# Small constants in one load, hH straight from x, and a front part with three engines' order written by hand

## The chip, the cores and the metric

One core of a Trainium2 chip runs the kernel. The metric is the device time of one execution in microseconds (us); before the change the median of three runs is 948.08 us (947.59 to 949.36).

## The reference

One layer of a hybrid backbone for two groups of tokens with the same weights: 128 prompt tokens and 512 latent tokens, 1024 channels. The part that the change touches is the beginning:

```python
def modulation(cond, w_ada, b_ada):
    mod = jax.nn.silu(cond) @ w_ada + b_ada
    return jnp.split(mod, 3, axis=-1)

def layer_forward(x, cond, ctx_kv, p):
    shift, scale, gate = modulation(cond, p["w_ada"], p["b_ada"])
    h = x * (1 + scale) + shift
    (v_h, x1, x0, g_h), (q, k, v, g_a), m = split_projection(h, p["w_in"], p["conv_w"], p["conv_b"])
    h_fwd, h_bwd = hyena_filters(x.shape[1], ...)
    y_h = hyena_long_conv(v_h, x1, x0, h_fwd, h_bwd, p["hyena_d"])
    ...

def hyena_filters(L, f_w1, f_b1, f_w2, f_b2, f_w3, f_freq):
    ...
    hf = jnp.sin(f_freq[0] * (z @ f_w1 + f_b1))
    hf = jnp.sin(f_freq[1] * (hf @ f_w2 + f_b2))
    hf = (hf @ f_w3).astype(jnp.float32).reshape(L, 2, D_HYENA)
    ...
```

Behind it come a gated long convolution by DFTs, a windowed attention with context keys, the merge of both branches, an output projection and a layer norm. All of it is in 32-bit floating point.

## The kernel before

**Layout.** Channels lie on the 128 partitions, tokens along the free axis: 640 columns, first the 128 of the prompt (PC), then the 512 latent ones (SC). The 1024 input channels are eight k-tiles. A weight tile `i` holds 128 output channels against all eight k-tiles (128 x 1024, 512 KB).

**Precision.** A 32-bit product is built from three matmuls. Each operand is split into a high half H, the value rounded to the matmul's format, and a low half L, the rest: `split` (L90-93) copies on ACT (ScalarE, L92) and subtracts on DVE (VectorE) or POOL (GpSimd) (L93). `accumulate` (L150-157) then runs, for one weight tile and one k-tile, the passes wh·hH, wh·hL, wl·hH, each in two halves of 320 columns: six matmuls at L154. In this text that is a tile-step, written as tile and k-tile (01: tile 0, k-tile 1). A whole tile is eight tile-steps.

**The front part, `prologue` (L240-310).** For each k-tile k it makes the modulation and the modulated input:

- two loads `ada` (512 KB each, one with the shift and one with the scale columns) into one of three buffers X, W, F in turn, so the loads of k+3 wait until the matmuls of k have read theirs; 16 small matmuls each, `adaT` (L235);
- `row` on ACT copies their sums out of PSUM (L267); four matmuls with `sel` turn them to one value per partition, `modT` (L285); DVE adds the bias, `mod` (L289);
- DVE makes `hx = x * scale + shift` from the load `xt` (L295); ACT copies it to `hH[k]` (L92); `hL[k]` is subtracted on POOL for even k and on DVE for odd k (L93).

Between these steps a `script` puts tile-steps of the tiles 0, 8 and 1 on TensorE (PE), as soon as their `hH`, `hL` and weight halves can be there. Tile 9 is loaded and split at the end, together with the first filter weights `w3`, the decays `dec` and the DFT matrices `draw`.

**The filter's two sine layers** (`hidden1`, `hidden2`, `sin_layer`, L195-218) are called whole at k=0 and k=1: two matmuls `ps_f` (L201), nine instructions on DVE (`arg`, `turns`, L202-207), a sine on ACT (L208). `hid` (L217, L218) is what the filters of all quarters are made of.

**What sets the order.** Inside `manual_schedule(engines={PE})` TensorE's instructions of the prologue stand as they are written; a scheduler orders the other engines, and everything behind the prologue, by its own estimate. All loads go through SP's queue in the order written (`keep_in_program_order` in `load_to`, L56-60), but for five small ones on ACT's queue (L184, L187). Landings are counted with eight semaphores used in turn, so a load is issued when the one eight places before it has landed.

**Small constants.** `cc`, `bss`, `sel`, `convw`, `hyd`, `ident` are loads of their own on SP, one put behind each of the first `ada` loads (`smalls`); `zemb`, `fw1`, `fs1`, `fw2`, `fs2` are loads on ACT's queue.

**Behind the prologue.** `quarter_head` runs tile 9, then the tiles 2, 10, 3, 11 and so on. From tile 2 on, `wtile` with `eng="dma"` writes -raw to `wl` on ACT (L132), adds the weights onto the rounded value by an accumulating load from POOL's queue (L133), and makes `wh` on ACT (L134). `dft_consts` splits the DFT matrices into `dftH`, `dftL`; `filter_spectrum(0)` starts with `w3s`, `w3h`, `w3l`, then the matmuls `fz` (L355) and `fl` (L365, L366), which read `hid`. `zs` (L447-451) are ACT's copies of a finished tile out of PSUM, `u` and `x` the short convolution.

Of the kernel before, what the change touches and what calls it, by code (L numbers as in the profile page):

```python
# [9 lines left out]
F32 = mybir.dt.float32  # L10
F32R = mybir.dt.float32r
AF = mybir.ActivationFunctionType
ALU = mybir.AluOpType
# [18 lines left out]
T_Q, T_K, T_V, T_GA, T_MH, T_MA, T_BH, T_BA, T_WO = 32, 40, 48, 56, 64, 72, 80, 88, 96  # L32

# [6 lines left out]
def tile_hyena_natten_step(ctx: ExitStack, tc: tile.TileContext, a, o):  # L40
# [55 lines left out]
    smalls = []  # L96

    def load(name, shape):
        out[name] = const.tile(shape, F32, tag=name, name=name)
        smalls.append((out[name][:], a[name]))  # L100

# [3 lines left out]
    cc = const.tile([P, NK, 2], F32, tag="cc", name="cc")  # L105
    load_to(cc[:], a["cc"])
# [4 lines left out]
    mod = const.tile([P, 2, NK, 2], F32, tag="mod", name="mod")  # L111
# [39 lines left out]
    def accumulate(ps, w, k, xh, xl):  # L151
        for wt, x, first, last in ((w[0], xh, True, False), (w[0], xl, False, False), (w[1], xh, False, True)):
            for hf in range(2):
                nc.tensor.matmul(  # L154
                    ps[hf][:, :HALF], wt[k], x[:, hf * HALF : (hf + 1) * HALF],
                    start=(first and k == 0), stop=(last and k == NK - 1), skip_group_check=True,
                )
# [13 lines left out]
    out = {"yh": {}}  # L171
# [10 lines left out]
    def hidden_loads():  # L182
        out["zemb"] = temp("u", "zemb", 4)[:33]
        nc.scalar.dma_start(out["zemb"], a["zemb"])  # L184
        for name, shape in (("fw1", [33, 64]), ("fs1", [64, 2]), ("fw2", [64, P]), ("fs2", [P, 2])):
            load(name, shape)
            nc.scalar.dma_start(*smalls.pop())  # L187


# [5 lines left out]
    def sin_layer(n, fs, w, src, dst):  # L195
        ar = temp("e", f"arg{n}")[:n]
        kr = temp("plus", f"turns{n}")[:n]
        for hf in range(2):
            hs = slice(hf * 320, hf * 320 + 320)
            ps = aux(f"ps_f{n}{hf}")  # L200
            nc.tensor.matmul(ps[:n, :320], w[:], src[:, hs], start=True, stop=True)  # L201
            nc.vector.tensor_scalar(ar[:, hs], ps[:n, :320], fs[:n, 0:1], fs[:n, 1:2], op0=ALU.add, op1=ALU.mult)  # L202
        nc.vector.tensor_scalar(kr, ar, 1.0 / (2 * math.pi), MAGIC, op0=ALU.mult, op1=ALU.add)
        nc.vector.tensor_scalar_add(kr, kr, -MAGIC)
        for c in (C1, C2, C3):
            nc.vector.scalar_tensor_tensor(ar, kr, -c, ar, op0=ALU.mult, op1=ALU.add)
        nc.vector.tensor_scalar(ar, ar, 3.1415925, -3.1415925, op0=ALU.min, op1=ALU.max)
        nc.scalar.activation(dst, ar, AF.Sin)  # L208

    def hidden1():  # L210
        out["hf1"] = temp("u", "hf1", 4)[:64]
        sin_layer(64, out["fs1"], out["fw1"], out["zemb"], out["hf1"])

    def hidden2():
        hf2 = temp("minus", "hf2")[:]
        sin_layer(P, out["fs2"], out["fw2"], out["hf1"], hf2)
        nc.scalar.activation(hid[:], hf2, AF.Copy)  # L217
        nc.vector.tensor_tensor(hid[64:], hf2[64:], f(hid[64:]), op=ALU.subtract)  # L218
# [3 lines left out]
    ccf = cc[:].rearrange("p k c -> p (k c)")  # L222
    nc.scalar.activation(th0[:], ccf, AF.Tanh, scale=0.5)
    nc.vector.scalar_tensor_tensor(th0[:], th0[:], 1.0, ccf, op0=ALU.add, op1=ALU.mult)
# [3 lines left out]
    def ada(ch, ps, raw):  # L228
        load_to(raw, a["wada"][ch])
        if smalls:  # L230
            load_to(*smalls.pop(0))
# [8 lines left out]
    def prologue():  # L240
        script = (
            ("", "", "", ""), ("00", "", "", ""), ("", "80", "01", "81"), ("", "", "02", "82"),
            ("", "10 11", "03", "83"), ("", "12 13", "04", "84"), ("", "14", "05", "85"), ("", "15", "06", "86 16 07 87 17"),
        )

        def work(k, step):
            for item in script[k][step].split():
                i, j = int(item[0]), int(item[1])
                accumulate(banks[i], early[i], j, hH[:, j], hL[:, j])
# [5 lines left out]
        hidden_loads()  # L255
        for n in ("bss", "sel"):
            load(n, a[n].shape)
        for n in ("convw", "hyd", "ident"):
            load(n, a[n].shape)
        for k in range(NK):  # L260
            psa = aux(f"adaT{k}")
            wt = hw.tile([P, 2048], F32, tag="XWFXWFXW"[k], name=f"ada{k}")
            for part in range(2):
                ada(part * 8 + k, psa[:, part * P : part * P + P], wt[:, 1024 * part : 1024 * part + 1024])
                work(k, part)
            row_ = hwa.tile([P, 2 * P], F32, tag="fb", bufs=2, name=f"row{k}")
            nc.scalar.activation(row_[:], psa[:, : 2 * P], AF.Copy)  # L267
            if k == 0:
                nc.vector.tensor_scalar_add(out["bss"][:, 1], out["bss"][:, 1], 1.0)
            xt = row(yhp, "yh", f"xt{k}")  # L270
            load_to(xt[:], a["xT"][:, k])
            if k == 0:
                begin(0)
            if k == 1:
                begin(8)
            if k == 2:
                w1 = [row(yhp, "yh", f"w1_{i}", F32R)[:, :512] for i in range(4)]
                begin(1, (w1[:2], w1[2:]), (aux("mm1lo"), aux("mm1hi")))
            if k == 7:
                w9 = hw.tile([P, 2, 1024], F32R, tag="X", name="w9")  # L280
                early[9] = wtile(9, dst=([w9[:, 0]], [w9[:, 1]]))
            work(k, 2)
            psm = aux(f"modT{k}")
            for c in range(2):
                nc.tensor.matmul(  # L285
                    psm[:, c * 2 : c * 2 + 2], row_[:, c * P : c * P + P], out["sel"][:, 0:2],
                    start=True, stop=True, skip_group_check=True,
                )
            nc.vector.tensor_tensor(  # L289
                mod[:, :, k, :], psm[:, 0:4].rearrange("p (s c) -> p s c", s=2),  # L290
                out["bss"][:, :, k : k + 1].to_broadcast([P, 2, 2]), op=ALU.add,
            )
            hx = hwa.tile([P, NT], F32, tag="cv", bufs=2, name=f"hx{k}")
            for c, s0, n in ((0, PC, LP), (1, SC, LS)):
                nc.vector.tensor_scalar(  # L295
                    hx[:, s0 : s0 + n], xt[:, s0 : s0 + n], mod[:, 1, k, c : c + 1], mod[:, 0, k, c : c + 1],
                    op0=ALU.mult, op1=ALU.add,
                )
            split(hH[:, k], hL[:, k], hx[:], nc.vector if k % 2 else nc.gpsimd)
            if k < 7:  # L300
                work(k, 3)
            if k == 0:
                hidden1()
            if k == 1:
                hidden2()
        load_filter(0)
        out["dft"] = hw.tile([P, 2560], F32, tag="F", name="draw")
        for i in range(2):
            load_to(out["dft"][:, i * 1280 : i * 1280 + 1280], a["dft"][:, i * 1280 : i * 1280 + 1280])
        work(7, 3)  # L310
# [32 lines left out]
    def filter_spectrum(q):  # L343
# [15 lines left out]
        hyd = out["hyd"][:, 2 * q : 2 * q + 2]  # L359
        nc.vector.scalar_tensor_tensor(hyd, pb0[:, :2], -DECAY0, hyd, op0=ALU.mult, op1=ALU.add)  # L360
# [135 lines left out]
    def long_conv(q):  # L496
        us, F, ident = out[f"u{q}"], out[f"F{q}"], out["ident"]

        def src(cls):
            ps = aux(f"ut{q}_{cls}")  # L500
            for i in range(2):
                s = us[i][:, GAP + cls : NG : 4] if cls < 4 else us[i][:, :LP]
                nc.tensor.transpose(ps[:, i * P : i * P + P], s, ident[:])  # L503
# [47 lines left out]
    def long_conv_back(q):  # L551
        us, ident, hyd, R, W = out[f"u{q}"], out["ident"], out["hyd"], out[f"R{q}"], out[f"W{q}"]
# [34 lines left out]
        for i in range(2):  # L587
            nc.tensor.transpose(outp[:, i * P : i * P + P], yp[:, i * P : i * P + P], ident[:])
        for i in range(2):
            up = us[i][:, :LP]  # L590
            nc.vector.scalar_tensor_tensor(
                up, up, hyd[:, 2 * q + i : 2 * q + i + 1], outp[:, i * P : i * P + P], op0=ALU.mult, op1=ALU.add
# [582 lines left out]
```

## Time and profile before

| what | us |
|---|---|
| median of three runs | 948.08 |
| the profiled execution | 949.61 |
| its span, first to last instruction | 947.7 |
| PE busy | 921.4 |
| DVE, ACT, POOL busy | 469.9, 375.8, 153.8 |
| first matmul starts | 5.75 |
| last tile-steps of the prologue start | 60.24 |
| tile 9 on PE | 63.44 to 70.74 |

The profile is one execution. Each row of a timeline has the start and duration in us, the engine, the line of the code, the operation, what is written from what (names without numbers) and its shape, the number of merged instructions, and in brackets how long the engine had been idle before it and what ended that. SPq, ACTq and POOLq are queues that issue loads; PEld is the load of weights into the array, which overlaps with matmuls. A table of stretches gives the busy time of each engine within it. PEclk is the share of the full TensorE clock that was granted. The loads of the front part, by issue and landing (us):

| load | issued | landed |
|---|---|---|
| first half of `ada` for k=0 | 1.17 | 5.61 |
| `xt` for k=0 | 5.63 | 9.04 |
| first half of `ada` for k=1 | 6.47 | 13.90 |
| second half of `ada` for k=6 | 31.22 | 35.74 |
| second half of `ada` for k=7 | 36.18 | 41.67 |
| `raw` of tile 2 | 39.82 | 47.90 |
| second half of `draw` | 43.31 | 51.85 |

### The profile page before, as it was taken

To read this page: it belongs to the slowest core of one execution; us is meant where nothing else is said; L and a number is where in the kernel's file an instruction comes from. 1 tells how busy PE (TensorE), PEld (TensorE's weight loads), DVE (VectorE), ACT (ScalarE), POOL (GpSimd) and SP (SyncE) were. 2 spreads that over 40 slices of the span, in tenths; PEclk is the share of its full clock that TensorE was granted. 3 is DMA by queue.
4 is the path that set the end of the run, shared out by engine and by line. 5 is a ranking of instruction groups with operands and counts; after the bars stand their busy time and mean duration, and the time that the engine had idled before them with its cause. 6 is when DMAs were issued, how large, how long until landed. Compare 5 with 4: busy or idle time off the path is not lost.

```text
span 947.7 us, 16408 instructions
## 1 busy us (share of the span) xinstructions
PE 921.4 (97%) x6732; PEld 868.3 (92%) x6732; DVE 469.9 (50%) x839; ACT 375.8 (40%) x759; POOL 153.8 (16%) x190
## 2 busy tenths in 40 slices
PE   5989999999999999999999999999999999999996
PEld 3889999999999999988888889989999999999885
DVE  5548685793795775333333332332271223325686
ACT  3266454554554324254444443443361112223300
POOL 1110010110110000464445544213100000000000
PEclk9899999999999999999999999999999999999999
DMA  8865564555565212322222221221212433223631
GB/s 314 315 174 117 125 142 100 134 133 117 119 141 120 71 56 73 113 80 70 68 74 68 63 68 54 76 70 46 68 52 82 135 133 112 72 84 108 204 111 67
DMA packets 38482, 102.57 MB, mean 108 GB/s; under 512 B 5287, under 2 KB 14951, under 8 KB 38408
## 3 DMA queue, kind: packets, MB, share of 16 engines
q1 hardware_dynamic: 33840, 86.69, 28.9%
q0 software_dynamic: 4032, 14.68, 9.5%
q8 instruction: 53, 0.87, 0.4%
q10 hardware_dynamic: 536, 0.16, 0.1%
q14 instruction: 21, 0.17, 0.1%
HBM read 97.85 MB, written 3.67 MB: 107 GB/s over the span
## 4 chain that ended last, share of the span: by engine, by line
PE 89%; DVE 2%; ACT 1%; DMA 1%; issue 0%; POOL 0%; POOLq 0%; DVEq 0%; ACTq 0%
PE mm L154 62%; PE out L1010 6%; PE v L680 5%; PE s L741 3%; PE o L785 3%; PE pt L778 2%; PE ve L689 1%; DMA raw<-wall 1%; DVE wl L93 1%; PE yb L142 1%; PE yb L143 1%; PE yb L141 1%; PE ut L503 0%; PE fl L365 0%; PE fl L366 0%; ACT wh L92 0%
## 5 line engine op out<-in xcount | busy, mean ns | idle before, releaser
L154 PE MATMUL mm<-hH,wh 128*128 128x320 f32 x1120 | 266.1, 317 | 2.2 <-ACT mh L883 1.1
L154 PE MATMUL mm<-hL,wh 128*128 128x320 f32 x1120 | 259.2, 310 | 2.1 <-POOL hL L93 2.1
L154 PE MATMUL mm<-hH,wl 128*128 128x320 f32 x1120 | 260.3, 311 | 0.8 <-DVE wl L93 0.8
L154 PEld LDWEIGHTS mm<-hH,wh 128*128 128x128 f32 x1120 | 185.9, 189 | 10.8 <-issue 6.9
L154 PEld LDWEIGHTS mm<-hL,wh 128*128 128x128 f32 x1120 | 188.7, 189 | 3.1 <-POOL hL L93 2.7
L154 PEld LDWEIGHTS mm<-hH,wl 128*128 128x128 f32 x1120 | 188.8, 189 | 2.2 <-DVE wl L93 1.6
L93 DVE TENSOR_TENSOR wl<-raw,wh 128x1024 fp32r<-128x1024 f32 x66 | 81.3, 1231 | 194.0 <-ACT wh L92 194.0
L92 ACT ACTIVATE wh<-raw 128x1024 fp32r<-128x1024 f32 x66 | 70.0, 1060 | 178.1 <-PE mm L154 99.6
L133 POOL DMA_DIRECT2D wl<-wall x28 | 24.4, 872 | 230.0 <-ACT wl L132 188.1
L762 POOL TENSOR_SCALAR p<-p,sm 128x384 f32<-128x384 f32 x32 | 43.7, 1376 | 46.8 <-DVE sm L761 46.8
L134 ACT ACTIVATE wh<-raw 128x1024 fp32r<-128x1024 f32 x28 | 29.7, 1062 | 46.6 <-PE mm L154 46.6
L780 ACT ACTIVATE pts<-pt 128x384 f32<-128x384 f32 x64 | 28.0, 491 | 35.9 <-PE pt L778 35.9
L1040 POOL TENSOR_TENSOR r<-r,bc 128x64 f32<-128x64 f32 x1 | 0.3, 319 | 249.5 <-ACT r L1039 249.5
L757 DVE CUSTOM_DVE_ANT_0 p<-s,tm 128x384 f32<-128x384 f32 x32 | 16.7, 556 | 44.6 <-PE s L741 44.6
L760 ACT ACTIVATE p<-p,sm 128x384 f32<-128x384 f32 x32 | 19.5, 612 | 47.0 <-DVE sm L757 47.0
L762 POOL TENSOR_SCALAR edge<-edge,sm 128x320 f32<-128x320 f32 x32 | 34.4, 1085 | 16.0 <-PE mm L154 8.8
L455 DVE SCALAR_TENSOR_TENSOR x<-zs,convw,x 128x641 f32<-128x641 f32 x32 | 28.3, 885 | 5.7 <-ACT x L453 5.6
L132 ACT ACTIVATE wl<-raw 128x1024 fp32r<-128x1024 f32 x28 | 30.1, 1076 | 2.0 <-DMA raw<-wall 2.0
L757 DVE CUSTOM_DVE_ANT_0 edge<-s,tm 128x320 f32<-128x320 f32 x32 | 14.6, 489 | 31.3 <-PE s L741 27.1
L154 PE MATMUL mm<-yhH,wh 128*128 128x320 f32 x128 | 29.9, 315 | 0.0
L741 PE MATMUL s<-k,q 64*128 64x320 f32 (+2 forms) x160 | 29.4, 461 | 0.0
L154 PE MATMUL mm<-yhH,wl 128*128 128x320 f32 x128 | 29.2, 310 | 0.1
(312 smaller groups left out, 1662.6 us busy)
## 6 DMA issues: line engine op xcount, KB each, us to landing
raw<-wall SPq DMA_DIRECT2D x96, 512.0 KB, 3.7
wl<-wall POOLq DMA_DIRECT2D x28, 512.0 KB, 5.7
ada<-wada SPq DMA_DIRECT2D x16, 512.0 KB, 6.3
gate<-wada SPq DMA_DIRECT2D x8, 512.0 KB, 3.7
wo<-wall SPq DMA_DIRECT2D x8, 512.0 KB, 3.7
xt<-xT SPq DMA_DIRECT2D x8, 320.0 KB, 6.6
dec<-decay SPq DMA_DIRECT2D x20, 128.0 KB, 3.4
x<-xB SPq DMA_DIRECT2D x5, 512.0 KB, 5.6
```

The lines of the kernel that those rows point to most:

```text
L92: hi = nc.scalar.activation(dst_h, src, AF.Copy)
L93: return hi, (eng or nc.vector).tensor_tensor(dst_l, src, f(dst_h), op=ALU.subtract)
L132: nc.scalar.activation(wl, raw[:], AF.Copy, scale=-1.0)
L134: nc.scalar.activation(wh, raw[:], AF.Copy)
L154: nc.tensor.matmul(ps[hf][:, :HALF], wt[k], x[:, hf * HALF : (hf + 1) * HALF], start=(first and k == 0), stop=(last and k == NK - 1), skip ...
L455: nc.vector.scalar_tensor_tensor(d, zs[:, c : c + NG], convw[:, i, c : c + 1], d, op0=ALU.mult, op1=ALU.add)
L680: nc.tensor.matmul(ps[:, t // 2, t % 2 * 256 : t % 2 * 256 + 256], x[:, k, P * t : P * t + P], wk, start=first and t % 2 == 0, stop=last, ...
L741: nc.tensor.matmul(dst, q[rows(h)], k[rows(h)], start=True, stop=True, skip_group_check=True)
L757: nc.vector.tensor_tensor_reduce(pv, s[h][:, : hi - lo], tm[h][:, lo:hi], 1.0, 3.0e38, ALU.add, ALU.min, accum_out=sm[:, 0:1])
L762: nc.gpsimd.tensor_scalar_mul(pv, pv, sm[:, 2:3])
L785: nc.tensor.matmul(dst, lhs, rhs, start=start, stop=stop, skip_group_check=True)
L1010: ins = nc.tensor.matmul(dst, m[k][:, c0 : c0 + P], w[:, c : c + n], start=(first and k == 0), stop=(last and k == NK - 1), skip_group_che ...
```

## The change

- **Pack.** Ten small constants (`cc`, `bss`, `sel`, `fs1`, `fs2`, `fw1`, `fw2`, `convw`, `hyd`, `ident`) become slices of one array of 128 x 462, loaded first of all on SP; `zemb` stays on ACT's queue. `bss` is copied out of it on DVE, 1 being added to the scale's half; `hyd` is made per quarter in a tile of its own.
- **hH.** ACT computes it from `xt` with scale and bias of `mod`, in two instructions (prompt, latent), and no longer copies `hx`; DVE still makes `hx`, and now `hL` for all k. `mod` is a small tile per k in four buffers.
- **Order.** `manual_schedule` covers PE, DVE and ACT. The weight loads of tiles 0, 8 and 1 (`wraw`) stay at their places in SP's queue, but their splits (`begin`) go behind `hH` and `hL` of the same k. The `script` has two places per k instead of four. In a prologue's tile-step the pass wh·hL comes last (`lead=(0, 2, 1)`).
- **Filter layers in pieces.** `sin_layer` becomes a generator; `layers` says how many of its pieces follow each k. The second layer's matmuls come at k=4, its sine and `hid` after the loop.
- **Head.** `quarter_head(0)` is taken three steps further ahead before the filter spectrum is woven in.

Instructions of later parts that the scheduler places can still stand between those of the prologue.

```diff
+PACK = (("cc", 16), ("bss", 16), ("sel", 2), ("fs1", 2), ("fs2", 2), ("fw1", 64), ("fw2", 128), ("convw", 96), ("hyd", 8), ("ident", 128))
...
-    cc = const.tile([P, NK, 2], F32, tag="cc", name="cc")
-    load_to(cc[:], a["cc"])
+    pack = const.tile([P, sum(n for _, n in PACK)], F32, tag="pack", name="pack")
+    load_to(pack[:], a["pack"])
...
-    def accumulate(ps, w, k, xh, xl):
-        for wt, x, first, last in ((w[0], xh, True, False), (w[0], xl, False, False), (w[1], xh, False, True)):
+    def accumulate(ps, w, k, xh, xl, lead=(0, 1, 2)):
+        passes = (w[0], xh), (w[0], xl), (w[1], xh)
+        for i in lead:
+            wt, x = passes[i]
...
+        for p, hs in zip(ps, halves):
+            nc.tensor.matmul(p[:n, :320], w[:], src[:, hs], start=True, stop=True)
+        for p, hs in zip(ps, halves):
+            nc.vector.tensor_scalar(ar[:, hs], p[:n, :320], fs[:n, 0:1], fs[:n, 1:2], op0=ALU.add, op1=ALU.mult)
+        yield
         nc.vector.tensor_scalar(kr, ar, 1.0 / (2 * math.pi), MAGIC, op0=ALU.mult, op1=ALU.add)
+        yield
...
         script = (
-            ("", "", "", ""), ("00", "", "", ""), ("", "80", "01", "81"), ("", "", "02", "82"),
-            ("", "10 11", "03", "83"), ("", "12 13", "04", "84"), ("", "14", "05", "85"), ("", "15", "06", "86 16 07 87 17"),
+            ("", ""), ("00", "01"), ("80", "81"), ("02", "82 10"), ("11", "12 03 83"),
+            ("13", "04 84 14"), ("05", "85 15"), ("06", "86 16 07 87 17"),
         )
+        layers = (1, 2, 2, 2, 1, 2, 3, 1)
...
             hx = hwa.tile([P, NT], F32, tag="cv", bufs=2, name=f"hx{k}")
             for c, s0, n in ((0, PC, LP), (1, SC, LS)):
...
+                cs = slice(s0, s0 + n)
+                nc.vector.tensor_scalar(hx[:, cs], xt[:, cs], mod[:, 1, c : c + 1], mod[:, 0, c : c + 1], op0=ALU.mult, op1=ALU.add)
+                nc.scalar.activation(hH[:, k, cs], xt[:, cs], AF.Identity, scale=mod[:, 1, c : c + 1], bias=mod[:, 0, c : c + 1])
+            nc.vector.tensor_tensor(hL[:, k], hx[:], f(hH[:, k]), op=ALU.subtract)
+            if k < 2:
+                begin((0, 8)[k])
...
+            work(script[k][1])
+            for _ in range(layers[k]):
+                next(filt, None)
+        now(filt)
...
-    with tc.manual_schedule(engines={mybir.EngineType.PE}):
+    with tc.manual_schedule(engines={mybir.EngineType.PE, mybir.EngineType.DVE, mybir.EngineType.Activation}):
         prologue()
     tc.keep_in_program_order(last[0])
     head = quarter_head(0)
     next(head)
     dft_consts()
-    weave(head, filter_spectrum(0), 2 + NK, N_FILTER)
+    for _ in range(3):
+        next(head)
+    weave(head, filter_spectrum(0), NK - 1, N_FILTER)
```

149 lines of the change are left out of this document (66 added, 83 removed).

## The prediction

> **What bounds the kernel now.** I read the page first (busy shares and the chain), then the stretches of the front part, then what TensorE waits for there, then single rows.
>
> ```profile
> PE 921.4 (97%) x6732; PEld 868.3 (92%) x6732; DVE 469.9 (50%) x839; ACT 375.8 (40%) x759; POOL 153.8 (16%) x190
> PE 89%; DVE 2%; ACT 1%; DMA 1%; issue 0%; POOL 0%; POOLq 0%; DVEq 0%; ACTq 0%
> ```
>
> TensorE (PE) is busy for 97% of the span and owns 89% of the chain, so an edit counts only if PE idles less or runs faster. The change leaves the matmuls as they are. What it can win lies where PE is not full, and of all its places the front, up to about 63 us, is the only one that the change touches. These are stretches of it (columns: stretch, its length, busy time of PE, weight loads, DVE, ACT, POOL, granted clock, DMA share, GB/s):
>
> ```profile
> 14.85:18.26 3.41, 3.18 (x30) 2.17 (x22) 2.62 (x4) 0.77 (x1) 0.00 (x0) 1.00 1.15 404
> 18.26:21.68 3.42, 1.26 (x7) 1.01 (x8) 2.49 (x5) 3.12 (x5) 0.00 (x0) 1.00 0.90 357
> 21.68:25.09 3.41, 3.41 (x36) 2.06 (x35) 3.17 (x6) 1.54 (x4) 0.00 (x0) 0.50 1.05 420
> 25.09:28.50 3.41, 3.41 (x15) 3.41 (x14) 3.26 (x5) 0.20 (x1) 0.00 (x0) 0.50 1.01 384
> 28.50:52.40 23.90, 21.43 (x266) 18.89 (x267) 9.54 (x21) 7.97 (x13) 4.15 (x3) 1.00 0.85 289
> 52.40:55.81 3.41, 2.08 (x14) 1.55 (x13) 2.28 (x4) 1.33 (x3) 1.54 (x1) 1.00 0.90 247
> 55.81:59.22 3.41, 3.41 (x15) 3.41 (x15) 1.79 (x4) 0.74 (x1) 0.00 (x0) 0.50 0.01 5
> ```
>
> Two things cost here: idle PE, and a halved clock in 21.68 to 28.50 and 55.81 to 59.22 (steps of 3.41 us). At half clock a 128x320 matmul follows the last one after 0.267 us (pairs start at 25.41 and 25.94), at full clock after 0.148 (pairs at 42.71 and 43.00): a microsecond at half clock does 0.55 us of work. After 62.9 the next 37 us hold 36.7 us of busy PE, so time won in the front stays won, unless something behind it gives it back. The waits of PE up to 70.74 us, the end of weight tile 9 (total, times, longest):
>
> ```profile
> PE adaT L235 <- DMA ada<-wada: 8.0, 3, 5.7
> PE modT L285 <- ACT row L267: 2.6, 3, 1.3
> PE mm L154 <- POOL hL L93: 2.1, 2, 1.1
> PE ps_f L201 <- ACT hf L208: 1.5, 1, 1.5
> ```
>
> **The change, part by part.**
>
> *Packed constants.* Loads are counted by eight semaphores in turn, so a ninth waits for the first to land. Before, the small loads take these: SP issues `sel` at 2.91 and `xt` only at 5.63, when the first `ada` (from 1.17) has landed at 5.61. The second `adaT` stage then waits on PE:
>
> ```profile
> 2.91 0.33 SPq L57 DMA_DIRECT2D sel<-sel  x1
> 5.63 0.33 SPq L57 DMA_DIRECT2D xt<-xT  x1
> 14.04 1.08 PE L235 MATMUL adaT<-ada,st 128*32 128x128 f32 x16 [1.98 <-DMA ada<-wada]
> ```
>
> With one load in their place the big loads follow each other from 1.2 us on; the 2.7 us stop goes, and with it the 1.98 us. Against it, `pack` (462 x 4 x 128 bytes = 237 KB for the 8 KB of `cc`) takes about 0.6 us at 400 GB/s ahead of the first `ada`: 0.5 us later, hiding nothing.
>
> *Filter layers in pieces.* The second layer's matmuls wait 1.55 us at 19.5 for the sine of the first. They move to k=4 with cover: 1.55 us saved, and their 1.89 us at half clock become 1.89 x 0.55 = 1.04, another 0.85.
>
> *Order on ACT.* `row` of k=1 stood behind a weight split that waited for its load (0.84 us of PE), `row` of k=6 behind `wl<-raw`, which waited for its load (1.26 us):
>
> ```profile
> 47.93 1.06 ACT L132 ACTIVATE wl<-raw 128x1024 fp32r<-128x1024 f32 x1 [2.03 <-DMA raw<-wall]
> 48.89 0.36 ACT L267 ACTIVATE row<-adaT 128x256 f32<-128x256 f32 x1
> 49.31 0.61 PE L285 MATMUL modT<-sel,row 128*128 128x2 f32 x4 [1.26 <-ACT row L267]
> ```
>
> `row` now goes ahead of the split, 0.84 + 1.26 saved. But the hand-written order does not cover `wl<-raw`, which belongs to a later part: in the changed instruction list it stands ahead of `row` of k=7. Its load is behind the last `ada` as before, landing at about 48 or earlier; PE, which reached the last `adaT` at 50.83, comes to it near 48. I cost this at 0, up to 2 if the load is later.
>
> *hH straight from x; hL on DVE, its pass last.* PE's two 1.07 us waits for POOL's `hL` (1.54 us there, 0.82 on DVE) and one of 0.27 for `hH` go: 2.4. ACT now writes `hH` in two Identity activations instead of one copy of 0.74. No row has this form; the nearest are `u` (128x641, scale and bias, 0.99) and the 128x128 copy (0.30), so 0.35 + 0.75 = 1.1, between 0.74 and 1.3. It no longer waits for `hx` (0.80).
>
> *Waits that come in.*
> - k=1: tile-step 01 now follows `modT` directly: `mod` 0.16, `hH` 1.1 and hand-overs of 0.04: 1.3 us of idle PE.
> - k=4: `row` stands behind the first sine on ACT. After `modT` of k=3 come `mod` 0.2, `hH` 1.1, `hL` 0.83, the last two filter steps 0.82 + 0.48, sine 0.74, `row` 0.39 and hand-overs 0.1: 4.7. PE has three tile-steps of six matmuls (0.9 each) and `adaT` (1.27) to do: 4.0. Wait 0.7; behind it in PE's queue stands everything.
> - k=7: `mod` stands behind filter work on DVE. After `modT` of k=6: 0.2 + 1.1 + 0.83, then one `arg` 0.82, `w3s` 0.84, two `arg` 1.64, `w3l`, then `mod` 0.2 and `hH` 1.1. PE meanwhile has five tile-steps, `adaT` and `modT`: 4.5 + 1.27 + 0.5 = 6.3. `w3l` has two prices:
>
> ```profile
> 53.80 1.58 DVE L93 TENSOR_TENSOR w3l<-w3s,w3h 128x512 fp32r<-128x512 f32 x1 [0.70 <-ACT w3h L92]
> 62.64 0.69 DVE L93 TENSOR_TENSOR sl<-sd,sh 128x512 fp32r<-128x512 f32 x1 [1.51 <-ACT sh L92]
> ```
>
> The first ran beside POOL's `hL`, the second alone; POOL has no such work any more, so 0.69: 7.4 - 6.3 = 1.1 of wait (2.0 with 1.58), and 0.3 for `hL` behind it: 1.4.
>
> *Behind the prologue.* `hid` is now made late, behind the `dft` splits. ACT has from the last `hH` on `w9` 1.05, 23 more pieces worth 11.8 (`zs`, `wh`, `u`, `dftH`, sine, `wl`, `ndH`, by their rows) and `hid` 0.72, DVE 0.83: 14.4. PE has from there the last three tile-steps (2.7, plus the 0.3 wait) and two whole tiles (7.3 each, the last at 63.44 to 70.74): 17.6. Covered by 3.2 us; cost 0, and a stall of what is beyond that if a load keeps ACT waiting. The 1.1 us of `fz` and first `fl` matmuls only change place.
>
> **The sum.** Waits before 28.5 us: out 1.98 + 0.84 + 1.55 = 4.37, in 0.5 + 1.3 = 1.8; net 2.57, worth 0.55 each while the clock is half: 1.4. After 28.5: out 1.26 + 2.14 + 0.27 = 3.67, in 0.7 + 1.4 = 2.1; net 1.5. Second layer at full clock: 0.85. Clock: PE idles less between 18 and 22, so the rise may come one step earlier, worth 3.41 x 0.45 = 1.5; even odds, 0.75. The drop at 55.81 followed a step with 2.08 us busy of 3.41; a 1.4 us wait falls into one step again, so I keep it. Total 4.5. The profiled execution took 949.6 us (span 947.7, 1.9 around it); it becomes 945.1. The median of the runs is 1.5 below it: 948.1 becomes **943.6**. With the bounds (clock one step later or two earlier, k=7 2.0, last `row` 2, none of the k=4 wait) this case spans 941 to 946.5.
>
> **Rivals.**
> 1. *The clock rises two steps earlier*, near 21.7: 3.0 instead of 0.75, **941.3**. For it: 18.26 to 21.68 ran full, after a step with 3.18 us busy; with its wait gone PE is busy in every step from 14 on. Against: 21.68 to 25.09 was busy throughout and the next step was still half. With the k=1 and k=7 waits near nothing too, 940. (The Trainium skill, TensorE: Matmul & The Clock Gate, part 1 on the HAM clock gate, has the rate double after one busy window of about 3.4 us. By that rule the rise comes here; the trace agrees at 18.26 and disagrees at 25.09.)
> 2. *The order by hand does not hold where it counts*: `row` of k=7 waits behind `wl<-raw` and DVE is slow beside POOL's queue. Before, this load landed 6.2 us after the last `ada`. Landing so after a late one, it costs 2.0, and k=7 another 0.9: **946.5**.
> 3. *Nothing is left*: what the front wins is given back behind it, since DVE stands idle for `hid` some 4 us and `wl`, `zs` and `sh` queue up on ACT; PE then stops at `fz` or `fa`. Speaking for it: DVE is 10.00 of 10 busy in 110 to 120. Against: only 53 of 70 us in 60 to 130. **948**.
> 4. *Slower: the clock stays half through the dense part.* Mixed `adaT`, `modT` and matmuls did not lift it at 25.09, and now this mixture lasts longer. Each step beyond 28.5 costs 1.5; from the third on (half until past 38.7) the gain is gone; five steps give 948.1 - 4.5 + 7.7 = **951.3**. Against: tile-steps of full matmuls did lift it at 28.50.
>
> **Chances.** Forecast 0.56, rival 1 0.10, rival 2 0.12, rival 3 0.08, rival 4 0.14, with any larger stall on `hid`. Less than 0.2% (1.9 us) can't be told from no change here. Faster 0.56 + 0.10 + 0.12 = 0.78, same 0.08, slower 0.14. The range leaves out most of rival 4 and the low end of rival 1: 939.0 to 949.5; the forecast's own is 941 to 946.5.
>
> **What would show it.** Right: no `adaT` wait near 14; no PE wait on POOL's `hL`; second layer's matmuls at k=4 in about 1.0; tile 9 ending near 65 (70.74 less 4.5 and the 1.1 us of `fz`); waits of about 1.3 behind the second `modT` and 1.4 at the last `hH`. Wrong: a clock of 0.50 after 32, `row` of k=7 after 49.5, a PE wait on `hid` near 70, or a full PE from 63 on with tile 9 ending at 69 or later.

## The result and the profile after

The changed kernel takes 951.30 us (median of 6 runs, 949.84 to 952.13), the kernel before 947.72 in runs beside it (6 runs, 946.55 to 949.36): ratio 1.0036, with an interval of 1.0023 to 1.0049. It is slower by about 3.5 us, where 943.6 was forecast, and outside the range of 939.0 to 949.5. Its profiled execution took 951.58 us, span 949.7.

The chain that ended last, of the changed kernel, is still PE's:

```profile
PE 92%; DVE 4%; ACT 1%; issue 1%; DMA 1%; POOL 0%; SPq 0%; POOLq 0%; ACTq 0%; DVEq 0%
```

In sum the front part did what was forecast. These are stretches of it and of what follows (columns as in the prediction: stretch, length, busy time of PE, weight loads, DVE, ACT, POOL, granted clock, DMA share, GB/s):

```profile
20.18:23.59 3.41, 3.41 (x38) 2.94 (x31) 0.92 (x3) 0.38 (x1) 0.00 (x0) 1.00 1.03 413
23.59:33.83 10.24, 8.04 (x105) 6.99 (x104) 7.44 (x14) 5.99 (x10) 0.00 (x0) 1.00 0.99 366
33.83:37.25 3.42, 3.42 (x15) 3.42 (x16) 1.79 (x4) 1.20 (x2) 0.00 (x0) 0.50 1.02 350
74.79:78.21 3.42, 3.42 (x13) 3.42 (x14) 2.03 (x3) 2.85 (x7) 0.33 (x1) 0.50 1.02 271
```

The clock comes up to stay, but for single steps, at 23.59 instead of 28.51 us (up to that record the column shows 1.00, but pairs of 128x320 matmuls start 0.53 us apart there, at 22.53 and 23.07, which is half clock; behind it 0.30). Tile 9 ends at 65.18, where 70.74 was and 65 was forecast. But a half-clock step stands at 74.79, in a stretch that ran full before. PE's waits over the whole span show what is new:

```profile
PE modT L271 <- ACT row L264: 2.7, 2, 2.2
PE mm L158 <- ACT hH L284: 2.6, 2, 1.5
PE fp L144 <- DVE sl L95: 2.2, 2, 1.1
PE mm L158 <- ACT zs L442: 1.7, 1, 1.7
```

The first two lie in the front and were forecast (in other sizes). The other two lie behind it: on `zs` at 74.79, and on `sl` near 178 and 254 us. To see what each is worth, I use PE's lag below: the time since the start of the span, less the usual distance of all matmuls begun until then (the median start-to-start distance of each form, over all profiles of this study). Only differences of it mean something: a lag that grows by 1 us is 1 us lost.

```
lag at (us)        66      70      80     170     182     258     300
before           32.74   32.63   32.63   32.81   32.88   32.92   32.84
after            28.07   28.10   31.46   31.52   33.52   35.51   35.69
```

At 66 us the changed kernel is 4.7 us ahead; it then loses 3.3 us near 75, 2.0 near 178 and 2.0 near 254, and is 2.9 behind at 300. This profile of the kernel before is of a long execution (949.61 us against a median of 947.72). Against a second one (`before_again` below, 947.30 us; lag 30.69 at 66 and 30.80 at 300) the lead is 2.6 and the deficit 4.9. What is lost between 66 and 300 us does not depend on which of the two is taken.

*The loss near 75.* PE's tile 10 needs the PSUM bank that held tile 9. PE had finished tile 9 at 65.18, but ACT's copies of it (`zs`) stand in ACT's queue behind `wh` of tile 3, which may not be written before PE is done with tile 2, and behind `wl` of tile 11. ACT and PE in the changed kernel's timeline (start, duration, what is done, idle time before it and its releaser):

```profile
71.96 1.06 ACT L136 ACTIVATE wh<-raw 128x1024 fp32r<-128x1024 f32 x1 [2.54 <-PE mm L158]
72.93 1.04 ACT L134 ACTIVATE wl<-raw 128x1024 fp32r<-128x1024 f32 x1
...
74.29 0.45 ACT L442 ACTIVATE zs<-mm 128x320 f32<-128x320 f32 x1
```

```profile
72.74 0.40 PE L357 MATMUL fl<-w3l,hid 128*128 128x512 f32 x1
74.79 0.90 PE L158 MATMUL mm<-hH,wh 128*128 128x320 f32 x2 [1.65 <-ACT zs L442]
```

The start at 74.79 comes 2.05 us after the last one instead of 0.23, and the half-clock step behind it costs 3.41 x 0.45 = 1.5: together 3.3. In the kernel before, the four copies of tile 9 stood ahead of that `wh`.

*The losses near 178 and 254.* In the filter spectrum of q=1 and q=2, `fp` has a pass on `sh`, then one on `sl`. Between them PE has only four transposes; before, 16 and 20 matmuls stood there (the four transposes and 12 and 16 matmuls of the projections). PE, and DVE, which makes `sl`:

```profile
177.88 0.66 PE L494 MATMUL ut<-pack,u 128*128 128x128 f32 x4
179.66 0.39 PE L144 MATMUL fp<-sl,dftH 128*128 128x256 f32 x1 [1.12 <-DVE sl L95]
```

```profile
176.22 0.71 DVE L362 TENSOR_TENSOR sd<-fl,dec 128x512 f32<-128x512 f32 x1
...
178.09 0.91 DVE L446 SCALAR_TENSOR_TENSOR u<-zs,pack,u 128x641 f32<-128x641 f32 x1
178.89 0.71 DVE L95 TENSOR_TENSOR sl<-sd,sh 128x512 fp32r<-128x512 f32 x1
```

DVE has four more operations between `sd` and `sl` and is never idle; PE waits 1.12 us for it.

The diff changes nothing in what these instructions do. What it alters ahead of them is when `hid` is made, here on ACT in the kernel before and in the changed one:

```profile
30.78 0.72 ACT L217 ACTIVATE hid<-hf 128x640 fp32r<-128x640 f32 x1
```

```profile
66.68 0.82 ACT L216 ACTIVATE hid<-hf 128x640 fp32r<-128x640 f32 x1
```

That is 36 us later. The first matmuls on it (`fz`) go from 59.33, ahead of tile 9, to 72.06, behind tile 2, and the scheduler arranges everything behind accordingly. **Theory:** the late `hid` costs what is lost behind 70 us, by the order that comes of it. **Rivals:** the parts in the front (pack, split from x, clock) cost it; or only one of the stalls hangs on `hid`; or the weave of the tiles with the filter spectrum costs it, which the diff also alters ("Head" in the list of changes).

### The profile page after: what moved, and what is told of

Read it like the earlier page. It is cut to its first block, busy times and chain, and to the rows that moved or that the text cites. A ratio compares the mean times of both kernels' runs of the same rounds, so it can differ in the third digit from the quotient of the medians.

```text
span 949.7 us, 16425 instructions
## 1 busy us (share of the span) xinstructions
PE 922.8 (97%) x6732; PEld 870.2 (92%) x6732; DVE 470.0 (49%) x844; ACT 377.4 (40%) x767; POOL 146.7 (15%) x186
## 4 chain that ended last, share of the span: by engine, by line
PE 92%; DVE 4%; ACT 1%; issue 1%; DMA 1%; POOL 0%; SPq 0%; POOLq 0%; ACTq 0%; DVEq 0%
PE mm L158 64%; PE out L1003 6%; PE v L673 5%; PE s L734 3%; PE o L778 3%; PE pt L771 2%; PE ve L682 1%; PE adaT L231 1%; ACT hH L284 1%; DMA ada<-wada 1%; PE yb L143 1%; PE yb L144 1%; PE yb L145 1%; PE gate L231 0%; DVE u L591 0%
## 5 line engine op out<-in xcount | busy, mean ns | idle before, releaser
L446 DVE SCALAR_TENSOR_TENSOR x<-zs,pack,x 128x641 f32<-128x641 f32 x32 | 28.3, 884 | 14.2 <-ACT x L444 14.0
L158 PE MATMUL mm<-yaH,wl 128*128 128x320 f32 x128 | 29.2, 309 | 0.0
```

Source lines behind the costliest of these rows:

```text
L158: nc.tensor.matmul(ps[hf][:, :HALF], wt[k], x[:, hf * HALF : (hf + 1) * HALF], start=(i == 0 and k == 0), stop=(i == lead[2] and k == NK - ...
L446: nc.vector.scalar_tensor_tensor(d, zs[:, c : c + NG], convw[:, i, c : c + 1], d, op0=ALU.mult, op1=ALU.add)
```

## The experiments

All are compared with the kernel before in runs on the same chip, where it took 947.1 to 947.7 us in the median. This table sets them side by side; its first column is where the full clock begins that lasts, with the start of later half-clock steps in brackets (all have one in the last 7 us).

```
                 full clock from            lag 66   lag 300   lag 450   median us
before           28.51 (55.81)              32.74    32.84     35.66      947.72
before_again     25.77 (53.08)              30.69    30.80     33.80      947.30 (one run)
pack_alone       26.51 (53.82)              30.69    31.18     33.80      947.06
x_alone          28.13                      30.39    30.51     33.39      947.47
hid_late         21.73 (49.03)              25.57    29.40     32.22      945.60
layer_k4         23.95                      25.90    26.01     28.88      941.50
k4_x             21.25                      22.90    23.06     25.88      940.66
k4_x_pack        21.84                      22.75    23.21     25.88      938.59
after            23.59 (33.83, 74.79)       28.07    35.69     37.86      951.30
lay_early        21.99 (32.23 to 39.06)     27.37    27.87     30.51      943.00
wh3_pool         24.50 (34.74)              28.66    33.78     38.28      951.03
pe_only          22.39                      24.52    25.07     27.71      941.23
pe_script        17.28                      18.94    19.54     21.99      935.90
script_by_hand   26.03                      24.81    25.36     28.15      941.28
script_late      15.02 (404.14)             19.69    23.66     31.04      944.18
```

### Is it the late hid?

**lay_early**: the changed kernel with the pieces of the second layer placed earlier.

```diff
-        layers = (1, 2, 2, 2, 1, 2, 3, 1)
+        layers = (1, 2, 2, 2, 2, 4, 2, 0)
```

> The changed kernel with one tuple altered: the pieces of the second filter layer stand earlier by hand, so that hid is made ahead of the last row of the front part instead of behind its loop. In the instruction list the first filter-spectrum matmuls then stand ahead of tile 9 again, the zs copies of tile 9 ahead of wh of tile 3, and 20 and 9 matmuls between the two passes of fp of q=1 and q=2 instead of 4 and 4. Theory (the late hid moves the rest by one tile, and that order gives back more than the front part wins): tile 9 ends near 65.5 as in the changed kernel, no PE wait on zs near 74 (3.3 us with the clock step behind it), fp waits on sl from 2.2 us to under 0.6 (about 4 us with hand-overs), time 943.5 to 945. Rival A (what the change put into the front, its pack, its hH and its clock step, costs the time; hid is a bystander): 950 to 952. Rival B (only the zs wait comes from hid; fp waits for another reason): 947 to 948.5.

Measured: 943.00 us (942.14 to 943.73), ratio to before 0.9949 [0.9937, 0.9961]. `hid` is made at 51.33. The waits on `zs` and `sl` are gone, and between 66 and 300 us the lag grows by 0.5 us only, against 7.6 in the changed kernel. The copies of tile 9 stand ahead of the `wh` again (ACT's timeline in this kernel):

```profile
70.74 0.46 ACT L442 ACTIVATE zs<-mm 128x320 f32<-128x320 f32 x1
...
74.61 1.06 ACT L136 ACTIVATE wh<-raw 128x1024 fp32r<-128x1024 f32 x1
```

One tuple gives 8.3 us, so neither pack nor split nor clock made the change slow. Rivals A and B fall. The altered weave is still in this kernel, and in pe_only and pe_script below, so by itself it does not cost the time either.

**pe_only**: the changed kernel, with PE's order alone by hand.

```diff
-    with tc.manual_schedule(engines={mybir.EngineType.PE, mybir.EngineType.DVE, mybir.EngineType.Activation}):
+    with tc.manual_schedule(engines={mybir.EngineType.PE}):
```

> The changed kernel with only PE's order of the front part written by hand; the scheduler orders DVE and ACT there, as before the change, and makes hid early by itself. Theory: the losses behind 70 us go as in lay_early, fp waits under 0.6 us, no zs wait near 74; the front keeps what the pack and the split from x give, but rows may queue again behind wl<-raw (1 to 2 us): 944 to 946.5. Rival A (pack, hH, clock cost the time): 950 to 952. Rival C (the hand order of DVE and ACT made the front gain): tile 9 ends at 68 or later and the time is 947 or more although fp does not wait.

Measured: 941.23 us (940.39 to 943.82), 0.9937 [0.9923, 0.9952]; better than expected. The scheduler makes `hid` at 45.40 by itself, nothing is lost behind 66 us, and the front is 2.9 us better than in lay_early (lag 24.52 against 27.37): the order by hand on DVE and ACT cost something there, instead of winning.

**hid_late**: the kernel before, with the second layer behind the loop.

```diff
-            if k == 1:
-                hidden2()
+        hidden2()
         load_filter(0)
```

> The kernel before with one call moved: the second filter layer whole behind the front loop instead of at k=1. In its instruction list the first filter-spectrum matmuls go from ahead of tile 9 to behind tile 2, and 4 and 4 matmuls stand between the passes of fp of q=1 and q=2, as in the changed kernel; but the zs copies of tile 9 stay ahead of wh of tile 3. Theory: the front wins 1.0 to 2.0 us (its wait of 1.55 at half clock and the second layer's matmuls at half clock go), the two fp stalls come in at about 2 us each, and no zs wait near 74: net 949 to 951 against 947.7. Rival A (hid is a bystander): 945.7 to 947.2, only the front's gain. Rival B (the fp stalls come from elsewhere in the change): no fp wait on sl over 0.6 us at q=1 and q=2, same time as in rival A.

Measured: 945.60 us (944.92 to 947.24), 0.9980 [0.9971, 0.9989]: just below the time that rival A named (945.7 to 947.2), for another reason. The two `fp` stalls are there as in the changed kernel (2.2 us in two waits on `sl`; the lag grows by 3.8 between 66 and 300 us), with nothing of the change in the kernel but the late `hid`, made at 64.59. The loss near 75 is not there; here the copies of tile 9 stand ahead of `wh`. What my expectation had wrong was the front: 1 to 2 us expected, 7.2 measured by the lag at 66 (32.74 to 25.57), or 5.1 against before_again.

### What is each part worth in the front?

**layer_k4**: the kernel before, the second layer at k=4.

```diff
-            if k == 1:
+            if k == 4:
                 hidden2()
```

> The kernel before with one number altered: the second filter layer at k=4 instead of k=1, neither packed constants nor split from x nor orders by hand; its instruction list behind the front part is that of before. Theory (moving the second layer off the dense early front lets the clock rise earlier, as hid_late showed with PE 7.2 us of work further on at 65 us, and an early hid keeps the order behind it): clock full from about 21.7, no fp waits, 940 to 942. Rival A (by the recorded sum the moved layer is worth 1.55 x 0.55 + 0.85 = 1.7 us): 945 to 946. Rival B (the gain of hid_late needs the layer to be behind the loop, because its DVE work at k=4 holds up hH): PE waits on hH of over 2 us at k=5, 944 to 946.

Measured: 941.50 us (940.80 to 942.89), 0.9935 [0.9921, 0.9949]: the theory's time. One digit gives 6 us. Of the change it takes only the place of the second layer's matmuls: no packed load, no split from x, no order by hand on ACT and DVE. Stretches of it:

```profile
20.54:23.95 3.41, 3.41 (x16) 3.41 (x14) 2.08 (x3) 1.56 (x4) 0.00 (x0) 1.00 1.03 404
47.84:51.26 3.42, 2.35 (x17) 2.08 (x16) 1.76 (x3) 0.85 (x3) 1.53 (x1) 1.00 0.92 207
```

PE is full in the step to 23.95 (its matmuls there still at half rate) and at full clock from then on; before, it waited 1.55 us for the sine until 21.03, and the full clock that lasts began at 28.51. The step 47.84 to 51.26 holds the last wait on POOL's `hL`; no half step follows it here.

**pack_alone**: the kernel before, with the packed constants only (the diff's PACK, its one load, `bss` and `hyd` in tiles of their own).

> The kernel before with the small constants packed into one load and nothing else of the change; same instruction list behind the front. Theory by the recorded sum: the adaT wait of 1.98 goes, first ada 0.5 later, net 1.5 at half clock = 0.8 us, 946.0 to 946.9. Rival D (hid_late has no such wait although it loads as before does: the wait is no work of the small loads): within 0.3 us of before, 947.0 to 947.6, the second adaT stage beginning near 12.1 as in hid_late. Rival E (with the loads denser the clock rises a step earlier): 944.5 to 945.7.

**x_alone**: the kernel before, with the split of the rows only.

```diff
-            split(hH[:, k], hL[:, k], hx[:], nc.vector if k % 2 else nc.gpsimd)
+                nc.scalar.activation(hH[:, k, cs], xt[:, cs], AF.Identity, scale=mod[:, 1, k, c : c + 1], bias=mod[:, 0, k, c : c + 1])
+            nc.vector.tensor_tensor(hL[:, k], hx[:], f(hH[:, k]), op=ALU.subtract)
```

> The kernel before with the split of the x rows altered alone: ACT writes hH from x in two activations and DVE makes hL; pass order, loads and filter layers as before. Theory by the recorded sum: POOL's hL waits of 1.07 and 1.07 and the hH wait of 0.27 go, a hH wait of about 1.3 at half clock may come in at k=1: 1.5 to 2.4 us, 944.9 to 945.8. Rival F (DVE, which now makes hL for every k beside the filter layer's arguments, is late with mod and hH, so new waits on hH or hL over 1 us come in at k=1 to k=3): 946.5 to 948.5.

**before_again**: the kernel before, profiled once more.

> The kernel before, profiled once more, to see which of its front waits recur. Theory by the recorded sum (small loads take the eight semaphores): the adaT wait of about 2 us near 14 is there again, the third ada landing 2.3 us behind the next load's issue. Rival D: no adaT wait over 0.5 us near 14, third ada landing near 11.4 as in hid_late, and the clock perhaps rising earlier; then the terms of the front part differ between executions of one kernel by 1 us or more.

Measured: pack_alone 947.06 us, 0.9992 [0.9983, 1.0000]; x_alone 947.47 us, 1.0003 [0.9995, 1.0012]: by itself the pack is worth 0.4 us at the edge of its interval (rival D's time), and the split nothing that can be seen. One wait tells why. PE's matmuls of the second layer in pack_alone, x_alone and before_again, in this order:

```profile
19.48 2.33 PE L200 MATMUL ps_f<-hf,pack 64*128 64x320 f32 x4 [1.99 <-ACT hf L207]
```

```profile
21.82 2.50 PE L201 MATMUL ps_f<-hf,fw 64*128 64x320 f32 x4 [3.88 <-ACT hf L208]
```

```profile
19.31 2.50 PE L201 MATMUL ps_f<-hf,fw 64*128 64x320 f32 x4 [2.22 <-ACT hf L208]
```

PE stops there for the first layer's sine, however early PE comes. In pack_alone and before_again ACT waits for DVE's chain of arguments before that sine (0.56 and 0.79 us). In before_again the wait for the third `ada` at 11.65 is 0.24 us, not 1.98 (that load landed at 11.51 instead of 13.90), and the wait for the sine is 2.22 instead of 1.55. So the 1.98 us that the prediction gave to the small loads belonged mostly to one execution, and what is won of it flows into the next wait. In x_alone the wait for the sine grows to 3.88 us, and there it is ACT's order that pushes the sine back:

```profile
18.52 1.20 ACT L297 ACTIVATE hH<-xt,mod 128x128 fp32r<-128x128 f32 x2 [1.65 <-DVE mod L289]
...
21.03 0.74 ACT L208 ACTIVATE hf<-arg 64x640 f32<-64x640 f32 x1
```

DVE has the argument ready at 18.94, only 0.45 us later than in before_again. But `hH` of k=1, which no longer waits for `hx`, now goes ahead of the sine, and so does the table load of 1.28 us that stands before it. In before_again the table load came at 16.45, behind `row`, and `hH` behind the sine. So the extra `hL` work on DVE, which the expectation of k4_x below blames, accounts for at most those 0.45 us. Rival F had the time right, but by waits on `hH` and `hL`; the wait was on the sine.

**k4_x** and **k4_x_pack**: layer_k4 with the split of x_alone, and with that and the pack.

> layer_k4 with the split straight from x added (ACT writes hH from x, DVE makes hL), nothing else of the change. Theory (x_alone won nothing because the wait for the first sine, then on the path at 19.5, grew from 2.2 to 3.9 us by the hL work on DVE; with the layer at k=4 that wait is gone): the three POOL hL waits of layer_k4 (2.4 us) go, 939.2 to 940.2. Rival F (DVE is late with hL and hH all the same, waits of 1.2 us in sum as in x_alone): 940.2 to 941.3. Rival G (the split from x is worth nothing anywhere): 941.3 to 942.

> k4_x with the packed constants added: all three parts of the change, but the second layer whole at k=4, no order by hand on DVE and ACT, passes and steps of PE as before. Theory (pack_alone won nothing since the same PE wait came 7 us later, at the first sine; that wait is not there any more, but the loads also landed in time without the pack): within 0.5 us of k4_x. Rival E (with the wait for the sine gone, the pack shows its worth of 0.8 to 1.9 us): 937.5 to 939.3.

Measured: k4_x 940.66 us (940.04 to 940.86), 0.9928 [0.9916, 0.9941]; k4_x_pack 938.59 us (937.72 to 939.29), 0.9905 [0.9890, 0.9920]. With the wait for the sine off the path the split seems worth something: lag 25.90 to 22.90 at 66 us in the profiles, though the medians lie only 0.8 apart, which the intervals do not tell from nothing. That is the time of rival F, and waits on `hL` and `hH` of 1.0 us in sum are left. For the pack it is the other way round: the lags agree (22.90 and 22.75), the medians differ by 2.1, and the intervals overlap a little. All four runs with the pack (up to 939.29) lie below all five without it (from 940.04), but the profiles are of the slowest of the four and the fastest of the five. So the pack seems to give something here, as rival E had it; how much, and where, stays open, for no row of the profiles shows it.

### The order by hand, and a version that beats both

**pe_script**: pe_only with one tile-step moved back to k=2.

```diff
-            ("", ""), ("00", "01"), ("80", "81"), ("02", "82 10"), ("11", "12 03 83"),
+            ("", ""), ("00", ""), ("80", "01 81"), ("02", "82 10"), ("11", "12 03 83"),
```

> pe_only with one tile-step (block 1 of tile 0) moved on PE from directly behind the modT of k=1 to behind that of k=2, as before the change. Theory: the wait of 2.79 us on hH at 19 and the half-clock step behind it (1.5 us) go in part, time from 941.2 to 938 to 940. Rival: PE comes to the next adaT earlier and waits there or at its row instead, 940.5 to 941.7.

Measured: 935.90 us (935.26 to 937.09), 0.9881 [0.9868, 0.9895]; more than expected, and the fastest of all. Stretches of it:

```profile
13.87:17.28 3.41, 3.41 (x37) 3.31 (x40) 3.38 (x6) 1.18 (x3) 0.00 (x0) 1.00 1.03 418
20.69:60.00 39.31, 38.91 (x383) 35.82 (x382) 26.26 (x47) 25.52 (x50) 2.76 (x3) 1.00 0.87 297
```

With no wait on `hH` at 19 PE is busy throughout, the clock is full from 17.28 up to the last 7 us, and from 20.69 to 60 PE idles 0.4 us in all.

**script_by_hand**: pe_script with DVE and ACT by hand too (layers as in lay_early).

> pe_script with DVE and ACT also in the order written by hand, in the form of lay_early (hid ahead of the last row). Theory (the hand-written order stalls PE at k=4, where row stands behind the first sine: 2.20 us in the changed kernel against 0.7 in the recorded sum, and a half-clock step or two behind it, 1.5 to 3 us): row of k=4 waits about 2 us again, 938.5 to 941 against 935.9. Rival (with the moved step PE reaches that row later, so it waits under 1 us): 935.5 to 937.

Measured: 941.28 us (940.32 to 942.03), 0.9935 [0.9921, 0.9948]: 5.4 us slower than pe_script, a little above what was expected, but by another wait. The `row` of k=4 waited 0.68, not 2. Instead PE's first tile-step of tile 8 waited for its weights:

```profile
18.70 0.56 PE L158 MATMUL mm<-hH,wh 128*128 128x320 f32 x2 [1.42 <-ACT wh L94]
```

By hand ACT makes that `wh` behind `hH` of k=1, at 17.61; in pe_script it does so ahead of it, at 13.85. The clock then came up at 26.03 instead of 17.28.

### Is it the lateness, or these two queues?

**wh3_pool**: the changed kernel, with one copy on POOL.

```diff
+            if i == 3:
+                nc.gpsimd.tensor_copy(wh, raw[:])
+            else:
+                nc.scalar.activation(wh, raw[:], AF.Copy)
-            nc.scalar.activation(wh, raw[:], AF.Copy)
```

> The changed kernel, hid as late as there, with one copy moved: wh of tile 3 is written by POOL instead of ACT. In the instruction list zs of tile 9 then stands behind no wh that waits for tile 2, though still behind wl of tile 11, and the fp passes of q=1 and q=2 get 11 and 9 matmuls of cover instead of 4 and 4. Theory (not the lateness of hid but the queue orders that come of it cost the time): the zs wait at 74.8 falls from 1.65 to under 0.5 us with no half clock behind it, fp waits on sl under 0.6 us, 951 goes to 943.5 to 946. Rival H (a late hid costs by itself, whatever the order, for DVE and ACT run late behind it): 949 to 951.

**script_late**: pe_script with the second layer behind the loop.

```diff
-        layers = (1, 2, 2, 2, 1, 2, 3, 1)
+        layers = (1, 2, 2, 2, 0, 0, 0, 0)
```

> pe_script with the pieces of the second filter layer all behind the front loop, so hid is late as in the changed kernel; the front itself keeps its order and DVE and ACT are the scheduler's. In the instruction list the first filter-spectrum matmuls stand behind tiles 9, 2 and 10, the zs copies of tile 9 ahead of wh of tile 3, 11 and 9 matmuls between the passes of fp of q=1 and q=2, as in wh3_pool. Theory (a late hid moves the filter spectrum behind by a tile or two, and the order that comes of it has waits of PE on zs, sl or ul behind 70 us, whichever front there is): 3 to 6 us lost behind 70, 939 to 942. Rival (in a front without stalls a late hid costs nothing, as the recorded sum had it): 935.3 to 936.7. Only the fp cover of 4 matmuls costs, not the lateness: also 935.3 to 936.7, with no wait over 0.6 us behind 70 us.

Measured: wh3_pool 951.03 us, 1.0041 [1.0029, 1.0054]; my theory expected 943.5 to 946 and missed, and the time is that of rival H. The `fp` waits are gone and the loss near 75 falls to 1.4 us with no half step behind it (lag 28.54 at 70, 29.93 at 80). But other waits came (PE's waits in wh3_pool, with the one on `zs` near 177 and that on `ul` near 261):

```profile
PE mm L161 <- ACT zs L445: 2.6, 2, 1.6
...
PE c_X L147 <- DVE ul L95: 1.4, 1, 1.4
PE pt L774 <- POOL edge L758: 1.2, 2, 0.7
```

script_late settles that a late `hid` costs time in another front too: 944.18 us (941.85 to 944.48, two of the five runs near 942), 0.9958 [0.9944, 0.9971], more than expected and 8.3 us behind pe_script with the same script of tile-steps (lag 19.69 against 18.94 at 66 us). Its waits are those of wh3_pool, in a kernel where behind the first loads no wait of PE in the front is over 1.0 us:

```profile
167.26 0.56 PE L158 MATMUL mm<-hH,wh 128*128 128x320 f32 x2 [1.63 <-ACT zs L442]
```

```profile
250.86 0.39 PE L144 MATMUL c_X<-ul,dftH 128*128 128x256 f32 x1 [1.41 <-DVE ul L95]
```

```profile
402.11 0.55 PE L771 MATMUL pt<-pack,edge 128*128 128x128 f32 x3 [0.73 <-POOL edge L755]
```

The last comes with three more on POOL's `pp` and `edge` and a half-clock step at 404.14: on POOL a mask addition that waits 3.76 us for its load stands ahead of `pp` and `edge`; in pe_script the additions in that place wait for DVE's `sm`, not for a load, and PE has none of these waits. So there is no one queue: in the four kernels with a late `hid` the order behind the front costs 4 to 8 us in sum, now in one place, now in another, and in those with an early one next to nothing up to 300 us. Why just these orders come of it was not followed further. That the order does it, and not the lateness as such (rival H), is read from the queue ahead of each single wait; no run has a late `hid` with the order of an early one, so this part is argued and not shown.

## Why the prediction was wrong

**The step that failed** is "Behind the prologue": `hid` made late, "cost 0", and "the 1.1 us of fz and first fl matmuls only change place". That step weighed whether `hid` itself would be in time, and it was: PE never waited on it. It did not ask what the move of `fz` (59.33 to 72.06) does to the order behind, which the scheduler lays out anew. The runs put 3.3 + 2.0 + 2.0 = 7.3 us there in the changed kernel, 8.3 by undoing it (951.30 to 943.00), and 8.3 by doing it to pe_script. The sum without this step came out: 943.6 forecast, 943.00 for lay_early, the changed kernel with an early `hid`; and 4.5 us forecast for the front, 4.7 by the lag at 66 against the execution that the sum was worked out from (2.6 against before_again). That is partly luck, since its terms were off both ways:

- *Packed constants*, 1.98 out and 0.5 in: pack_alone gives 0.4 us at the edge of its interval. The wait differed between executions of one kernel (1.98 and 0.24), and PE stood at the sine next anyway.
- *Second layer*, 1.55 x 0.55 + 0.85 = 1.7 with 0.75 for the clock: 6.0 us by layer_k4, more than twice as much. The clock came up 4.6 us earlier (23.95 instead of 28.51; at 0.45 us lost in each microsecond of half clock an estimated 2.1 us; against before_again it is 1.8 us earlier, 0.8 us), the half step at 55.81 went as well (1.5), and the waits ahead of it shrank. How the 6.0 us divide among these was not measured. Its matmuls took 1.34 at k=4, forecast 1.0.
- *Order on ACT*, 0.84 + 1.26 saved: the scheduler's order did as well or better (in pe_script PE waits for `row` 0.5 us in all); by hand it cost 2.9 us of lag (lay_early against pe_only) and 5.4 us (script_by_hand against pe_script).
- *hH from x, hL on DVE*, 2.4 out: nothing seen alone, since on ACT `hH` of k=1 went ahead of the sine; 0.8 (medians) to 3.0 (lag) once the second layer is away.
- *Waits that come in*: k=1 1.49 (1.3 forecast), k=7 1.10 (1.4), k=4 2.20 (0.7). The last was mis-sized because `mod` of k=3 did not start behind `modT` (27.5) but at 29.10: by hand, two `arg` operations stood ahead of it on DVE. Its 1.6 us on top of the 4.7 of the working give 2.3 of wait.
- *The signs named*: no `adaT` wait near 14, no wait on POOL's `hL`, tile 9 at 65.18: as forecast. A half clock after 32 was named as a sign against; it came (33.83) for one step, behind that 2.20 us wait.

Rival 1 (clock two steps earlier) did not come in the changed kernel. Rival 2's place did not stall: `row` of k=7 stands behind `wl<-raw`, but at 50.70 it waited for PE's own `adaT`, not for that load. Rival 3 was the nearest: given back behind the prologue, with `zs` and `wl` queued on ACT, as it said. It had the price (948) and the place (`fz` or `fa`) wrong, and was discounted because DVE was busy in only 53 of 70 us from 60 to 130; the waits came at single points in a queue, which a share over 70 us does not show. Rival 4 named the time that came, 951.3, by chance: its cause did not come, for the dense part ran at full clock from 23.59 but for one step.

## What to carry to other kernels

When a part of a program is moved and a scheduler orders the rest, the price of the move can lie in the order of the rest: ask of the new instruction list, for every pair that has to be covered (the two `fp` passes: 16 and 20 matmuls before, 4 and 4 after) and every queue with a waiting instruction (the `zs` copies behind a `wh` that waits for PE), whether it is still so, also 100 us behind the edit. A wait is worth only what the next wait on the same engine leaves of it: taking out the waits for `ada` or for `hL` alone gave 0.4 us or nothing while PE still waited for the sine, and moving that one call by three steps gave 6 us alone. In this kernel an order by hand did best on PE alone, the engine that bounds it; on DVE and ACT it put work ahead of what PE needed next.

## What the runs showed of the hardware

- Ahead of its first record the granted-clock column shows 1.00 while PE runs at half rate, and not in the changed kernel alone. In the kernel before pairs of 128x320 matmuls start 0.53 us apart at 15.75 and 16.28, in a stretch that the prediction shows with 1.00; in layer_k4 pairs of 128x320 matmuls start 0.53 us apart from 21.20 to 22.80, in a step shown as 1.00, and 0.30 apart from 24.37 on. The rate has to be read from the matmuls there.
- Steps of 3.41 us are counted from a phase that differs between executions, and the same wait falls in one step or is split between two. The kernel before had its first lasting rise at 28.51 in one execution and at 25.77 in another.
- How long the clock stays down differed. After the drops at 33.83 and 74.79 of the changed kernel, and at 49.03 of hid_late, one half step of full PE was enough; in the kernel before 21.68 to 25.09 was full too, as was 19.69 to 23.10 in pack_alone, and in both the next step was still half. (The Trainium skill, TensorE: Matmul & The Clock Gate, Part 1: The HAM clock gate, has one busy window raise the rate: the first three agree, the last two do not.)
- How little work brings a drop is not settled by these traces. Drops followed steps in which PE was busy for 1.21 and 1.76 of 3.41 us (the changed kernel, ahead of 33.83 and 74.79), 1.91 (script_late, ahead of 404.14), 2.08 (before, ahead of 55.81) and 2.41 (hid_late, ahead of 49.03). None followed one with 1.78 (script_late, 165.21 to 168.62, where PE waited 1.63 us) or 2.35 (layer_k4, 47.84 to 51.26). So a wait of 1 to 2 us may cost a half-clock step or not.
